# Encoder step on one core: token sums of squares pair by pair, the roots' broadcast ahead of the first ada products, 32-column products side by side

## Chip, cores, metric

The kernel runs on one core of a Trainium2 chip, as one launch. The metric is the device time in microseconds, and the kernel before takes 1043.99 us (median of three runs).

## What is computed

One step of an encoder with three kinds of mixers, for 512 prompt tokens and 64 sample tokens of width 2048, in fp32. What matters here is the beginning:

```python
mod = jax.nn.silu(c) @ w_ada + b_ada
shift, scale, gate = jnp.split(mod, 3, axis=-1)
h = rmsnorm(x, norm_g) * (1.0 + scale[:, None]) + shift[:, None]
proj = h @ w_in
```

`rmsnorm` divides each token by the root of the mean of its 2048 squares. Behind the projection come chunked attention, a state space branch, a pooling branch, a gated output projection and a last norm. The change touches none of these.

## The kernel before, in words

**Layout.** x stands feature-major: 16 blocks of 128 features (`xc`, four tiles of four blocks each) by 576 tokens, prompt first. It is loaded by 8 DMAs of two blocks each on the SP queue. An fp32 product on TensorE shows in the trace as two passes (two MATMUL and two LDWEIGHTS records). Projections are made as three products of rounded halves instead: weights and h are split into a high part and the rest (fp32r), and high x high, rest x high and high x rest are added in PSUM.

**Start (L346 to L399).** Each block of x is squared (ScalarE at L353 and L359, the last block on VectorE), and VectorE adds the squares of the even and the odd blocks into two accumulators `acc` (by the helper `add`, L67). Twelve products of `ident` with x (`warm`, L368), whose result nobody reads, run on TensorE meanwhile. Then TensorE sums over the 128 partitions (`pss`, L373): for each of five groups of 128 tokens, two products with `acc` as the stationary operand and one column of ones as the moving one. `rms_inv` (L100) makes the inverse root with one Newton step. Five diagonal matrices `dg` (L391) times ones spread it over all partitions (`rb`, L393 and L395), and ScalarE copies it to `rstdx` (L398, L399).

**Modulation of block b.** `ada_mm` (L330) multiplies SiLU(c) with 2048 x 256 weights of the modulation in 16 fp32 products. Each takes 32 columns of the array and writes 32 partitions of PSUM; four such column groups run side by side. `ada_sel` copies the four partial sums to SBUF (L336), transposes them (L338) and adds them up on VectorE (L340 to L343). `modulate` makes x times scale times `rstdx` (L76), the sample's h `hs` (L421), the prompt's high part `hh` (L423) and the rest `hl` (L76).

**First tiles (L429 to L443).** Of the input projection six tiles of 128 columns are made block by block while the modulation goes on: tiles 0 to 5 for the prompt (three products each, L436 to L438, into `fA` to `fD`), and "tile 6", the sample's 64 tokens for all six, as four fp32 products of 32 array columns each (`fS`, L442). `F1CUT` cuts the seven tiles of a block into three parts: ahead of the next block's ada products, between these and their selection, and behind it.

**Order.** From L320 to L689 the order on TensorE, SP, VectorE and ScalarE is the one in which the code is written (`manual_schedule`). The instructions ahead of L320 (constants, `ones` at L82, `pre` at L89) are placed among them by the framework's scheduler, and so is what comes behind L689. `pre` loads ScalarE's table for the root ahead of its use.

**Loads.** SP issues the loads of ada weights (2 x 1 MB a block, L189) and of first-tile weights (384 KB a block, L178) two blocks ahead. Two of three blocks use four buffers `ada`, so their loads wait for `ada_mm` of three blocks before.

Of the kernel before, what the change touches and what calls it, by code (L numbers as in the profile page):

```python
# [9 lines left out]
F32 = mybir.dt.float32  # L10
# [22 lines left out]
PRE = 2  # L33
F1CUT = ((6, 0), (1,), (2, 3, 4, 5))
MANUAL = 0
# [4 lines left out]
LASTENG = ("PE", "DVE", "Activation")  # L40
WARM = 12
WLANE = 0
W1POS = 2
# [5 lines left out]
def kernel(ctx, tc, xp, xs, xT, cT, wada_ss, wada_g, bsh, bsc, bgate, ng, wf1, wrest,  # L49
# [27 lines left out]

    # ---------------------------------------------------------------- constants
    ident = const.tile([128, 128], F32, name="ident")
# [8 lines left out]
    pre = const.tile([128, 1], F32, name="pre")  # L88
    A.activation(pre, ones[:, 0:1], AF.Sqrt)  # L89
    xc = [ck(f"xc{c}") for c in range(4)]  # L90
# [9 lines left out]
    def rms_inv(pool, ssq, n, bias, hbias, shape, tag):  # L100
        """1/sqrt(ssq/n + bias), with a Newton step; hbias is -bias/2, bias may be None"""
        v = pool.tile(shape, F32, tag=tag + "v", name="v")
        s = pool.tile(shape, F32, tag=tag + "s", name="s")
        ts(v, ssq, -0.5 / n, hbias, ALU.mult, ALU.add)
        if bias is None:
            A.activation(s, v, AF.Sqrt, scale=-2.0)
        else:
            A.activation(s, ssq, AF.Sqrt, scale=1.0 / n, bias=bias)
        r = pool.tile(shape, F32, tag=tag + "r", name="r")
        V.reciprocal(r, s)  # L110
        mul(s, r, r)
        mul(s, s, v)
        stt(r, s, 1.5, r, ALU.add, ALU.mult)
        return r

    # ---------------------------------------------------------------- PSUM
    psctx = ExitStack()
# [5 lines left out]

    # ---------------------------------------------------------------- weights: loaded ahead, split into high and low
    wsrc = [wrest[r, :, 8 * h:8 * h + 8] for r in range(38) for h in range(2)]
# [34 lines left out]

    # ---------------------------------------------------------------- startup: x, modulation, first tiles
    hh, hl = [], []
# [183 lines left out]
    for b in range(PRE):  # L346
        load_ada(b)
    # 1/rms of each token, on every partition
    acc = [wp.tile([128, NT], F32, tag="wh", name="acc") for _ in range(2)]
    for n in range(16):  # L350
        xv = xc[n // 4][:, n % 4]
        if n < 2:
            A.activation(acc[n], xv, AF.Square)  # L353
        else:
            sq = wp.tile([128, NT], F32, tag=("wl", "wr")[n % 2], name="sq")
            if n == 15 and 1:
                mul(sq, xv, xv)
            else:
                A.activation(sq, xv, AF.Square)  # L359
            if n < 16:  # L360
                add(acc[n % 2], acc[n % 2], sq)
            else:
                acc.append(sq)
    V.tensor_scalar(prm[:, 1], prm[:, 1], 1.0, None, op0=ALU.add)
    # keeps the array's clock up until the sums below
    warm = pp.tile([128, 2, 512], F32, tag="pj", name="warm")
    for n in range(WARM):
        PE.matmul(warm[:, 0, 0:128], ident, xc[3][:, WLANE, 0:128], start=True, stop=True)  # L368
    pss = mtile("pss", (128, 8))
    for t in range(5):  # L370
        t0 = 128 * t if t < 4 else NT - 128
        for n, a in enumerate(acc):
            PE.matmul(pss[:, t:t + 1], a[:, t0:t0 + 128], ones[:, 0:1], start=n == 0, stop=n == len(acc) - 1)  # L373
    ada_mm(0, 0)
    ada_mm(0, 1)
    r = rms_inv(s1, pss[:, 0:5], D, None, -0.5 * EPS, [128, 5], "n")
# [12 lines left out]
    rstdx = s1.tile([128, NT], F32, tag="rstdx", name="rstdx", bufs=1)  # L389
    for t in range(5):  # L390
        V.tensor_scalar(dg[:, t], ident, r[:, t:t + 1], None, op0=ALU.mult)  # L391
        if t < 4:
            PE.matmul(rb[:, 0, 128 * t:128 * t + 128], ones, dg[:, t], start=True, stop=True)  # L393
        else:
            PE.matmul(rb[:, 1, 0:64], ones, dg[:, t, 64:128], start=True, stop=True)  # L395
    split_w(0)
    ada_sel(0)
    A.copy(rstdx[:, NP:NT], rb[:, 1, 0:64])  # L398
    A.copy(rstdx[:, 0:NP], rb[:, 0])  # L399

    fA = pp.tile([128, 2, 512], F32, tag="pj", name="fA")
# [27 lines left out]
    def first_tiles(b, fs):  # L429
# [3 lines left out]
        for f in fs:  # L433
            if f < 6:
                wsl = slice(128 * f, 128 * f + 128)
                PE.matmul(f1p[f], wh[:, wsl], hh[c][:, i, 0:NP], start=f0, stop=False)  # L436
                PE.matmul(f1p[f], wl[:, wsl], hh[c][:, i, 0:NP], start=False, stop=False)
                PE.matmul(f1p[f], wh[:, wsl], hl[c][:, i, 0:NP], start=False, stop=l0)  # L438
            else:
                # the sample tokens token-major: a column group for each half of the tokens and of the features  # L440
                for g in range(4):
                    PE.matmul(fS[32 * g:32 * g + 32], hs[:, 32 * (g // 2):32 * (g // 2) + 32],  # L442
                              w[:, 384 * (g % 2):384 * (g % 2) + 384], start=f0, stop=l0, skip_group_check=True)  # L443
# [3 lines left out]
    for b in range(KT):  # L447
# [4 lines left out]
        if b == KT - 2:  # L452
            for n in range(3):
                w_load()
        first_tiles(b, F1CUT[0])
        if b + 1 < KT:
            ada_mm(b + 1, 0)
            ada_mm(b + 1, 1)
        first_tiles(b, F1CUT[1])
        if b + 1 < KT:  # L460
            ada_sel(b + 1)
            modulate(b + 1)
        if b == KT - 2:
            for n in range(1):
                w_split()
        first_tiles(b, F1CUT[2])
        if b == 0:
# [16 lines left out]

    # a projected tile: pieces (psum view, first token, count)
    def f1_pieces(f):
# [4 lines left out]
    def proj_steps(done):  # L491
        """one projected tile, a yield after each sixteenth; then done(psum)"""
        ps = pp.tile([128, 2, 512], F32, tag="pj", name="pj")
# [21 lines left out]
    def interleave(gens, units, total):  # L515
        """runs the steps of gens with the units spread over the first `total` of them"""
        n, done = 0, 0
# [9 lines left out]

    # ---------------------------------------------------------------- attention
    at = ExitStack()
# [192 lines left out]

    # ---------------------------------------------------------------- S5 branch, with the gates z beside it
    zs = ExitStack()
# [4 lines left out]
    def branch_rstd(tiles, ssq, width, out):  # L729
        """out[:, t] = 1/sqrt(sum over features / width + eps), on every partition"""  # L730
        v, s = tiles
# [24 lines left out]
    def s5_units(q):  # L756
# [3 lines left out]
        def op_x():  # L760
            ER = ck("ER", F32, (128, 2304))
            bc = ER[:, 1728:2240].rearrange("p (z a c) -> p z a c", z=4, a=4)
            for z, src in enumerate((sbr, sbi, scr, sci)):
# [4 lines left out]
                      E=[ER[:, 576 * z:576 * z + 576].rearrange("p (a j) -> p a j", a=4) for z in range(3)])  # L768
            # X[state, s, (g, c)] = a^(3-s) coef b
            X = s5.tile([128, 2, 4, 4, 32], F32, tag="X", name="X")  # L770
# [16 lines left out]
        def op_c():  # L787
            # C[state, tau, (g, c)] = c a^tau (imaginary part negated)
            tA, tB, bc = t_["tA"], t_["tB"], t_["bc"]
# [7 lines left out]
        def op_e(part):  # L797
            # E_j = e^(i phi (j+1)); the third row holds the decay, with resets
            E, tA, tB = t_["E"], t_["tA"], t_["tB"]
# [13 lines left out]
        def op_k():  # L813
            # taps of the chunk's own inputs: K[(f, g, c), tau, (g, c')], the skip added to tap 0
            X, Ct = t_["X"], t_["Ct"]
# [13 lines left out]
        def op_g(fp):  # L829
            # inputs of the chunks, rotated  # L830
            E, tA, tB, XT = t_["E"], t_["tA"], t_["tB"], t_["XT"]
# [73 lines left out]

    # pooling
    cinv = zp.tile([128, 16], F32, name="cinv")
# [135 lines left out]

    # ---------------------------------------------------------------- output projection and final norm
    pf = ctx.enter_context(tc.tile_pool(name="pf", bufs=8, space=PSUM, reuse_waits="tile"))
# [104 lines left out]
    def out_gate(t, po, n, cs=slice(0, 512)):  # L1150
        """x + gate * product"""
        out_mul(t, po, n, cs)
# [6 lines left out]
    def out_sum(t):  # L1159
        """the mean of the first three sums of squares, with eps, and that times -1/2"""  # L1160
        m = 128 if t < 4 else 64
# [10 lines left out]
    def out_scale(t, r, c, act=False):  # L1172
        """columns 512 c on: times r, and in the last group times the gain"""
        xv = xo[t][0:128 if t < 4 else 64, 512 * c:512 * c + 512]
# [22 lines left out]

    # in the last group the tiles end one after the other, the last one in two halves
    po = {t: pf.tile([128, 512], F32, tag="f", name="po2") for t in range(5)}
# [56 lines left out]
def _layout(i):  # L1256
# [31 lines left out]

    # groups g = 2 (4 f + q) + g2 -> partition (g2, state), column (q, f)
    def gs(a):  # L1290
        r = a.reshape((4, 4, 2) + a.shape[1:])          # f q g2 s ...
        return np.moveaxis(r, [2, 3, 1, 0], [0, 1, 2, 3])  # g2 s q f ...

# [68 lines left out]
```

## Time and profile before

| | |
|---|---|
| three runs | 1044.51, 1043.99, 1043.70 us |
| median | 1043.99 us |
| the profiled execution: span from the first to the last instruction | 1042.7 us; no other time of it is given |
| TensorE busy | 1011.0 us |
| VectorE, ScalarE busy | 710.5, 460.3 us |
| mean granted clock of TensorE | 0.993 |

Times in the trace count from the start of the span. A row of the timeline gives the start, the duration, the engine, the line, the operation, what it writes and reads, and how many instructions are merged in it. PE is TensorE, DVE VectorE, ACT ScalarE, SPq the queue of SyncE. The ends of matmuls are modelled, so the spacing of starts says more of their pace than a duration does. The granted clock is a share of 2.4 GHz.

### The profile page before, as it was taken

To read this page: it belongs to the slowest core of one execution; us is meant where nothing else is said; L and a number is where in the kernel's file an instruction comes from. 1 tells how busy PE (TensorE), PEld (TensorE's weight loads), DVE (VectorE), ACT (ScalarE), POOL (GpSimd) and SP (SyncE) were. 2 spreads that over 40 slices of the span, in tenths; PEclk is the share of its full clock that TensorE was granted. 3 is DMA by queue.
4 is the path that set the end of the run, shared out by engine and by line. 5 is a ranking of instruction groups with operands and counts; after the bars stand their busy time and mean duration, and the time that the engine had idled before them with its cause. 6 is when DMAs were issued, how large, how long until landed. Compare 5 with 4: busy or idle time off the path is not lost. (4 is left out here: it accounts for less than half of the span.)

```text
span 1042.7 us, 17908 instructions
## 1 busy us (share of the span) xinstructions
PE 1011.0 (97%) x7048; PEld 904.0 (87%) x7048; DVE 710.5 (68%) x1678; ACT 460.3 (44%) x913; POOL 4.2 (0%) x36
## 2 busy tenths in 40 slices
PE   4999999999999999999999999999999999999996
PEld 3556579999999999999989999998999988888885
DVE  5476777656454655645589797886444669988786
ACT  5232355546344535444653644657453513222325
POOL 0000000000000000000000000000000000000000
PEclk8999999999999999999999999999999999999999
DMA  9998833233232233222212322221322596746525
GB/s 365 411 352 327 325 116 116 89 93 98 80 110 84 87 104 99 72 82 73 66 60 81 92 81 71 76 79 42 102 81 82 172 307 207 227 157 192 151 91 192
DMA packets 51572, 148.44 MB, mean 142 GB/s; under 512 B 9313, under 2 KB 18529, under 8 KB 46817
## 3 DMA queue, kind: packets, MB, share of 16 engines
q1 hardware_dynamic: 51488, 147.31, 42.8%
q8 instruction: 55, 0.90, 0.4%
q14 instruction: 29, 0.23, 0.1%
HBM read 137.75 MB, written 9.53 MB: 141 GB/s over the span
## 5 line engine op out<-in xcount | busy, mean ns | idle before, releaser
L500 PE MATMUL pj<-hh,wh 128*128 128x288 f32 x1344 | 299.0, 304 | 0.5 <-DVE Q L76 0.5
L500 PE MATMUL pj<-hh,wl 128*128 128x288 f32 x1344 | 287.8, 296 | 0.0
L500 PE MATMUL pj<-hl,wh 128*128 128x288 f32 x1344 | 287.3, 295 | 0.0
L500 PEld LDWEIGHTS pj<-hh,wh 128*128 128x128 f32 x1344 | 214.6, 189 | 5.5 <-issue 0.8
L500 PEld LDWEIGHTS pj<-hh,wl 128*128 128x128 f32 x1344 | 216.0, 188 | 0.1
L500 PEld LDWEIGHTS pj<-hl,wh 128*128 128x128 f32 x1344 | 215.7, 188 | 0.1
L146 ACT CAST wh<-w 128x1024 fp32r<-128x1024 f32 x120 | 125.8, 1050 | 198.3 <-PE po L1122 86.2
L70 DVE TENSOR_TENSOR wl<-w,wh 128x1024 fp32r<-128x1024 f32 x120 | 146.6, 1222 | 94.0 <-ACT wh L146 93.0
L1119 PE MATMUL po<-wl,yh 128*128 128x512 f32 (+1 forms) x256 | 99.1, 387 | 0.0
L1120 PE MATMUL po<-wh,yl 128*128 128x512 f32 (+1 forms) x256 | 99.0, 387 | 0.0
L1118 PE MATMUL po<-wh,yh 128*128 128x512 f32 (+1 forms) x256 | 98.7, 387 | 0.0
L76 DVE SCALAR_TENSOR_TENSOR acc<-ada,scT,acc 128x512 f32<-128x512 f32 x120 | 83.0, 744 | 0.5
L621 ACT ACTIVATE P<-P,s 128x128 f32<-128x128 f32 (+4 forms) x80 | 43.3, 541 | 77.2 <-DVE s L620 76.9
L618 DVE CUSTOM_DVE_ANT_0 P<-sps,Tb 128x128 f32<-128x128 f32 (+4 forms) x80 | 36.5, 458 | 36.7 <-PE sps L614 22.6
L1118 PEld LDWEIGHTS po<-wh,yh 128*128 128x128 f32 x256 | 48.1, 188 | 9.9
L1120 PEld LDWEIGHTS po<-wh,yl 128*128 128x128 f32 x256 | 48.1, 188 | 9.8
L1119 PEld LDWEIGHTS po<-wl,yh 128*128 128x128 f32 x256 | 48.1, 188 | 9.8
L622 DVE RECIPROCAL s<-s 128x1 f32<-128x1 f32 (+1 forms) x80 | 12.8, 161 | 43.1 <-ACT P L621 42.4
L623 DVE TENSOR_SCALAR P<-P,s 128x128 f32<-128x128 f32 (+4 forms) x80 | 29.5, 370 | 2.3
L423 ACT ACTIVATE hh<-xc,m 128x512 fp32r<-128x512 f32 (+1 forms) x32 | 15.4, 528 | 34.4 <-DVE xc L76 34.4
L67 DVE TENSOR_TENSOR ssqa<-ssqa,sq 128x576 f32<-128x576 f32 x7 | 5.3, 756 | 35.8 <-ACT sq L666 35.8
L70 DVE TENSOR_TENSOR K<-kv,K 64x704 fp32r<-64x704 f32 x32 | 28.2, 883 | 0.5
(338 smaller groups left out, 1427.0 us busy)
## 6 DMA issues: line engine op xcount, KB each, us to landing
w<-in_wrest_dram SPq DMA_DIRECT2D x84, 512.0 KB, 3.7
ada<-in_wada_ss_dram SPq DMA_DIRECT2D x22, 1024.0 KB, 7.1
w<-in_wout_dram SPq DMA_DIRECT2D x32, 512.0 KB, 4.2
ada<-in_wada_g_dram SPq DMA_DIRECT2D x32, 512.0 KB, 4.4
adac<-in_wada_ss_dram SPq DMA_DIRECT2D x10, 1024.0 KB, 11.2
w<-in_wf_dram SPq DMA_DIRECT2D x16, 384.0 KB, 8.1
xc<-in_xT_dram SPq DMA_DIRECT2D x8, 576.0 KB, 7.3
Tb<-in_ext_dram SPq DMA_DIRECT2D x8, 512.0 KB, 3.9
```

The lines of the kernel that those rows point to most:

```text
L70: V.tensor_tensor(o, a, b, op=ALU.subtract)
L76: V.scalar_tensor_tensor(o, in0=a, scalar=s, in1=b, op0=op0, op1=op1)
L146: A.copy(wh, t)
L423: A.activation(hh[c][:, i, tk], xv[:, tk], AF.Identity, bias=m4[:, t:t + 1])
L500: PE.matmul(ps[:, ch, 0:HC], ws[:, k % 8], hs[c][:, i, HC * ch:HC * ch + HC], start=(k == 0 and first), stop=(k == KT - 1 and last))
L618: V.tensor_tensor_reduce(out=p[0:n, 0:nk], in0=ps[0:n], in1=Tb[0:n, h, ::-1][:, b0:b0 + nk], scale=1.0, scalar=-3.0e38, op0=ALU.add, op1=A ...
L621: A.activation(p[0:n, 0:nk], p[0:n, 0:nk], AF.Exp, bias=s4[0:n, 1:2], accum_out=s4[0:n, 2:3])
L622: V.reciprocal(s4[0:n, 3:4], s4[0:n, 2:3])
L623: V.tensor_scalar(p[0:n, 0:nk], p[0:n, 0:nk], s4[0:n, 3:4], None, op0=ALU.mult)
L1118: PE.matmul(po[t], yh[c][:, ci, s_], wh[:, i], start=f0, stop=False)
L1119: PE.matmul(po[t], yh[c][:, ci, s_], wl[:, i], start=False, stop=False)
L1120: PE.matmul(po[t], yl[c][:, ci, s_], wh[:, i], start=False, stop=l0)
```

## The change

It has three parts and some small ones with them. The squares of two blocks are added to each other at once, and the sum goes to TensorE, pair by pair, as five products with one column of ones, all 8 pairs accumulated in one PSUM tile; the accumulators are gone, and instead of 12 warming products in a row there is one behind each pair. Blocks 5, 10 and 15 are squared on VectorE. The broadcast of the roots comes ahead of the ada products of block 0, with the sample's diagonal first, and the split of the first weights comes behind the selection. `F1CUT` becomes two cuts, one for block 0 and one for the others, in which the sample's products stand directly ahead of the ada products. `pre` no longer reads `ones`.

```diff
-F1CUT = ((6, 0), (1,), (2, 3, 4, 5))
+F1CUT = (((6, 0, 1), (2,), (3, 4, 5)), ((6,), (0,), (1, 2, 3, 4, 5)))
-WARM = 12
-WLANE = 0
+WARM = 1
...
-    A.activation(pre, ones[:, 0:1], AF.Sqrt)
+    V.memset(pre, 1.0)
+    A.activation(pre, pre, AF.Sqrt)
...
-    acc = [wp.tile([128, NT], F32, tag="wh", name="acc") for _ in range(2)]
-    for n in range(16):
-        xv = xc[n // 4][:, n % 4]
-        if n < 2:
-            A.activation(acc[n], xv, AF.Square)
+    pss = mtile("pss", (128, 8))
+    warm = pp.tile([128, 2, 512], F32, tag="pj", name="warm")
+    for n in range(0, 16, 2):
+        sq = []
+        for m in range(n, n + 2):
+            q = wp.tile([128, NT], F32, tag=("wl", "wr")[m % 2], name="sq")
+            xv = xc[m // 4][:, m % 4]
+            if m in (5, 10, 15):
+                mul(q, xv, xv)
             else:
-            sq = wp.tile([128, NT], F32, tag=("wl", "wr")[n % 2], name="sq")
-            if n == 15 and 1:
-                mul(sq, xv, xv)
-            else:
-                A.activation(sq, xv, AF.Square)
-            if n < 16:
-                add(acc[n % 2], acc[n % 2], sq)
-            else:
-                acc.append(sq)
+                A.activation(q, xv, AF.Square)
+            sq.append(q)
+        add(sq[0], sq[0], sq[1])
+        for t in range(5):
+            t0 = 128 * t if t < 4 else NT - 128
+            PE.matmul(pss[:, t:t + 1], sq[0][:, t0:t0 + 128], ones[:, 0:1], start=n + t == 0, stop=n == 14,
+                      skip_group_check=True)
+        for w in range(WARM):
+            PE.matmul(warm[:, 0, 0:128], ident, xc[n // 4][:, n % 4, 0:128], start=True, stop=True)
     V.tensor_scalar(prm[:, 1], prm[:, 1], 1.0, None, op0=ALU.add)
-    warm = pp.tile([128, 2, 512], F32, tag="pj", name="warm")
-    for n in range(WARM):
-        PE.matmul(warm[:, 0, 0:128], ident, xc[3][:, WLANE, 0:128], start=True, stop=True)
-    pss = mtile("pss", (128, 8))
-    for t in range(5):
-        t0 = 128 * t if t < 4 else NT - 128
-        for n, a in enumerate(acc):
-            PE.matmul(pss[:, t:t + 1], a[:, t0:t0 + 128], ones[:, 0:1], start=n == 0, stop=n == len(acc) - 1)
-    ada_mm(0, 0)
-    ada_mm(0, 1)
     r = rms_inv(s1, pss[:, 0:5], D, None, -0.5 * EPS, [128, 5], "n")
...
-    for t in range(5):
+    for t in (4, 0, 1, 2, 3):
         V.tensor_scalar(dg[:, t], ident, r[:, t:t + 1], None, op0=ALU.mult)
...
-    split_w(0)
-    ada_sel(0)
     A.copy(rstdx[:, NP:NT], rb[:, 1, 0:64])
     A.copy(rstdx[:, 0:NP], rb[:, 0])
+    ada_mm(0, 0)
+    ada_mm(0, 1)
+    ada_sel(0)
+    split_w(0)
...
-        first_tiles(b, F1CUT[0])
+        cut = F1CUT[b > 0]
+        first_tiles(b, cut[0])
         if b + 1 < KT:
             ada_mm(b + 1, 0)
             ada_mm(b + 1, 1)
-        first_tiles(b, F1CUT[1])
+        first_tiles(b, cut[1])
...
-        first_tiles(b, F1CUT[2])
+        first_tiles(b, cut[2])
```

The rest of the diff takes out comments.

## Rows read from the trace of the kernel before

**Rows 1.** The page, busy time, share of the span and instructions of each engine.
```profile
PE 1011.0 (97%) x7048; PEld 904.0 (87%) x7048; DVE 710.5 (68%) x1678; ACT 460.3 (44%) x913; POOL 4.2 (0%) x36
```
**Rows 2.** Stretches: length, busy time of each engine, granted clock, DMA share, GB/s.
```profile
39.01:46.41 7.40, 7.40 (x62) 4.50 (x61) 3.68 (x10) 2.04 (x5) 0.00 (x0) 1.00 1.02 417
```
**Rows 3.** Timeline of ScalarE and VectorE, 5 to 9 us.
```profile
5.16 1.25 ACT L353 ACTIVATE acc<-xc 128x576 f32<-128x576 f32 x2 [2.30 <-DMA xc<-in_xT_dram]
...
7.44 1.43 DVE L67 TENSOR_TENSOR acc<-acc,sq 128x576 f32<-128x576 f32 x2 [4.29 <-ACT sq L359]
8.78 0.22 DVE L82 TENSOR_SCALAR onesr<-ident 128x128 fp32r<-128x128 f32 x1
```
**Rows 4.** Timeline of TensorE from its first product to the first sample products.
```profile
13.99 4.39 PE L368 MATMUL warm<-xc,ident 128*128 128x128 f32 x24 [13.99 <-DMA xc<-in_xT_dram]
...
19.27 2.90 PE L373 MATMUL pss<-onesr,acc 128*128 128x1 f32 x18 [0.77 <-DVE acc L67]
22.10 3.64 PE L330 MATMUL pa<-ada,sc 128*32 128x256 f32 x32
25.67 1.94 PE L393 MATMUL rb<-dg,onesr 128*128 128x128 f32 x8
...
27.61 0.39 PE L338 MATMUL pa<-ident,S 128*128 128x128 f32 x2
29.49 0.85 PE L442 MATMUL fS<-w,hs 128*32 128x384 f32 x8 [1.49 <-DVE hs L421]
```
**Rows 5.** Timeline of TensorE in three short stretches: the last passes of each.
```profile
16.90 1.38 PE L368 MATMUL warm<-xc,ident 128*128 128x128 f32 x10
...
20.30 1.87 PE L373 MATMUL pss<-onesr,acc 128*128 128x1 f32 x9
...
20.54 1.63 PE L373 MATMUL pss<-onesr,acc 128*128 128x1 f32 x7
```
**Rows 6.** Stretches of the start, columns as in rows 2.
```profile
19.30:20.50 1.20, 1.20 (x11) 1.20 (x12) 0.00 (x0) 0.00 (x0) 0.00 (x0) 1.00 0.95 385
20.60:23.90 3.30, 3.30 (x28) 2.37 (x31) 1.28 (x8) 0.93 (x2) 0.00 (x0) 0.50 1.04 429
30.80:34.10 3.30, 3.20 (x19) 1.59 (x23) 1.91 (x3) 1.01 (x3) 0.00 (x0) 0.50 1.06 382
```
**Rows 7.** Timeline of VectorE and ScalarE, 22 to 29 us.
```profile
22.20 0.16 DVE L73 TENSOR_SCALAR v<-pss 128x5 f32<-128x5 f32 x1 [2.90 <-PE pss L373]
...
23.47 1.07 DVE L391 TENSOR_SCALAR dg<-ident,r 128x128 f32<-128x128 f32 x5
24.45 0.95 DVE L70 TENSOR_TENSOR w1l<-w,w1h 128x768 fp32r<-128x768 f32 x1
28.11 0.17 DVE L340 TENSOR_REDUCE m<-pa 128x4 f32<-128x16 f32 x1 [2.71 <-ACT rstdx L398]
...
25.80 0.37 ACT L336 COPY S<-pa 128x256 f32<-128x256 f32 x1 [2.48 <-PE pa L330]
```
**Rows 8.** Timeline of TensorE in block 1, from the sample products to the ada products.
```profile
39.01 0.85 PE L442 MATMUL fS<-w,hs 128*32 128x384 f32 x8
...
39.35 0.51 PE L442 MATMUL fS<-w,hs 128*32 128x384 f32 x4
...
39.79 0.50 PE L436 MATMUL fA<-hh,w1h 128*128 128x512 f32 x1
40.12 0.39 PE L437 MATMUL fA<-hh,w1l 128*128 128x512 f32 x1
40.36 0.40 PE L438 MATMUL fA<-hl,w1h 128*128 128x512 f32 x1
40.68 1.93 PE L330 MATMUL pa<-adac,sc 128*32 128x256 f32 x32
```
**Rows 9.** SP's timeline, and the landing of the same loads (tile ada, 27.5 to 31 us).
```profile
27.67 2.80 SPq L189 DMA_DIRECT2D ada<-in_wada_ss_dram  x2
...
DMA to landing us min/median/max: 9.9/9.9/10.0
```

## The prediction

> **What bounds the kernel now.** I read the page's busy times first, then the stretches of time, then the timeline of single engines at the start. TensorE is busy 97% of the span [rows 1]. In one turn of the first loop (the 16 k-blocks that make the modulation and the first six tiles) it is busy for 7.40 of 7.40 us at the full granted clock [rows 2]; I take the other blocks of the loop for its like. So time taken off TensorE in a turn leaves the kernel's time one for one, and a delay ahead of the loop is carried to the end, since nothing behind it starts at a set time. What stands ahead of the loop is a chain, not an engine: x lands, squares, sums, root, broadcast, modulation, first product at 29.49 us [rows 4]. The reader is to see two things there: how fast a pass of TensorE with one moving column goes, and at which clock.
>
> An fp32 product is two passes in the trace. Passes that load 128 columns of weights follow each other every 0.208 us at the slow pace (14 passes of the warming products from 13.99 to 16.90) and every 0.223 us in the last seven passes of the sums (20.54 to 22.10); I use 0.213. At the fast pace it is 0.114 us (nine passes from 19.27 to 20.30) [rows 4, 5]. The pass of a sum moves one column and still takes as long as one that moves 128: the weights set it.
>
> **The clock.** The granted clock was 1.00 while sums ran from 19.3 to 20.5, fell to 0.50 (1.2 of 2.4 GHz) at that point, and stayed at 0.50 from 20.6 to 23.9 although TensorE's row is busy for all of those 3.30 us, first with sums, then with ada products [rows 6]. It had risen behind 2.9 us of warming products that move 128 columns [rows 5]. (The column prints 1.00 from the start of the trace; the pace of the warming passes shows the lower level until 16.9.) So passes of one column neither held nor raised it here.
>
> **The change, part by part.**
>
> 1. Sums on TensorE pair by pair. Removed: 14 additions, two accumulators, 20 passes behind the last addition, 24 warming passes. Added: for each of 8 pairs of squares one addition, 5 products of one column and one warming product, so 12 passes. At the slow pace a pair needs 12 x 0.213 = 2.55 us, at the fast pace 1.37. x brings a pair every 1.47 us (the first is there at 5.16, the seventh at 13.99, both starts released by x's DMA) [rows 3, 4]. At the slow pace TensorE is therefore the bound of the start, and only 2 of 12 passes move 128 columns. By the rows above I expect the slow pace throughout. The first pass needs the ones, written at 8.78 for 0.22 us behind the second addition [rows 3]: start at 9.0. The other end: if the ones come behind the first addition, two squares end at 5.16 + 1.25, an addition takes 0.72, the ones 0.22, so 7.4. I take 9.0, the place it has now. The last pass of a sum is the 94th: 9.0 + 93 x 0.213 = 28.8 us. Now it is at 20.54 + 6 x 0.213 = 21.8 us. **Later by 7.0 us** (5.4 with the early start).
>
> The additions that go from VectorE, the squares that move between ScalarE and VectorE, and the table for the root, whose load no longer has to wait for the ones, cost or bring nothing in this case: TensorE lies behind them. The squares now turn over three buffers each, so the squares of the last pair wait for TensorE to finish the fifth pair (9.0 + 5 x 2.55 = 21.8); a square and an addition later is still ahead of 26.9, when TensorE comes to that pair. Behind a held square on its engine stands nothing but other squares and the root.
>
> 2. Broadcast ahead of the ada products. Now the ada products of block 0 (22.10, 3.64 us) run under the root's chain (22.20 to 23.47), and the split of the first weights (24.45, 0.95 us on VectorE) runs under them too [rows 4, 7]. Afterwards all of it is in a row, from the last pass of the sums: 0.38 to the first VectorE step, 1.27 for the root, 0.33 for the first diagonal and its hand-over (five diagonals take 1.07), 10 passes 2.13, ada products until the copy 3.70 (22.10 to 25.80), copy 0.37, hand-over 0.10, transposes until the reduction 0.50 (27.61 to 28.11), modulation until the first sample product 1.38 (28.11 to 29.49). The split now stands in VectorE's order between the small parameters and the modulation, which adds its 0.95. Sum 11.1 us, against 29.49 - 21.82 = 7.7 us now: +3.4. If the clock rises as the ada products start, they take 1.93 instead of 3.64 [rows 4, 8]: +1.7. I take the middle, **+2.6**. Loads: SP issues none of its DMAs elsewhere in its order, but the reload of the first ada buffers waits for these products. It goes at 27.67 now, its second half by 30.5, and lands 9.9 later, at 40.4 [rows 9]; its use is at 40.68 + 7.40 = 48.1 [rows 2, 8]. Load and use both move by about 9 us, so the nearly 8 us of slack stay, and the small loads behind it on SP keep theirs.
>
> 3. The 32-column products side by side. In blocks 1 to 14 the sample products (fS) are followed by the ada products at once, without tile 0 between them. What leaves a turn [rows 8]: from fS to fA 0.44 (39.35 to 39.79) against 0.34 between two rounds of fS: 0.10; the first full product 0.33 against 0.24 for the next: 0.09; from fA to pa 0.32 against 0.24: 0.08. Together 0.27, times 14: **-3.8 us**. The hand-over from fS to pa is in no row; it costs between nothing and those 0.27, which would leave no gain. I take nothing, since both sides work in the same form; the Trainium skill (TensorEngine Tiling (Array Packing), Key Properties) has the engine drained by a change of mode and not by a change of tile, and no row here shows that hand-over. The modulation of the next block gets a tile more of cover, so nothing new waits. Block 0 has the order changed without the two groups meeting: 0, give or take 1.0 for where the low clock of 30.8 to 34.1 [rows 6] comes to lie.
>
> Sum: 7.0 + 2.6 - 3.8 = +5.8 us on the span of 1042.7, which gives 1048.5. The page has no other time of that execution; the median of the runs, 1043.99, lies 1.3 above the span, and on it the sum is **1049.8 us**. Own range of this case: down by 1.6 (early start), 0.9 (clock rises early) and 1.0 (block 0) to 1046.3; up by 0.8, 1.0 and half of part 3 to 1053.5.
>
> **Rivals.**
>
> A. Faster: the clock rises early in the sums and stays. TensorE then works without a break from 9.0 on; if it got the high level after as long as the warming products did, 14 passes go at 0.213 (3.0 us) and 79 at 0.114: last pass at 21.0, 0.8 earlier than now. The broadcast is 1.0 and the ada products 1.7 shorter than in part 2: +0.7 instead of +3.4. The 3.3 us at 0.50 in block 0 would be half as long: -1.6. With part 3: -0.8 + 0.7 - 1.6 - 3.8 = -5.5, 1038.5 us. It decides itself at the second or third pair: with the high clock a pair (1.37) keeps up with x. For it: TensorE would be busy from 9 us on, with a warming product in each pair. Against it: the fall at 20.5 in the midst of sums and no rise in the busy 3.3 us behind it [rows 6]. The Trainium skill (TensorE: Matmul & The Clock Gate, Why this matters for your kernels) speaks for it: keep the engine busy without gaps and it reaches the full clock. By that rule the time would be this 1038.5; the rows show a busy engine at 0.50, which is why I give it less. Chance 0.20.
>
> B. No measurable difference: the clock rises half way through the sums. 46 passes at 0.114 instead of 0.213 take 4.6 off: 1045.2. Chance 0.10.
>
> C. The change does not do in part 3 what it says: the form changes within the group cost as much as the two that go. Then 1049.8 + 3.8 = 1053.6. For it: the ada products start anew with other weights, and the passes of a round share their start. Chance 0.07.
>
> **How the numbers follow.** The likeliest case has 0.63. Slower by over 0.2% (2.1 us, about what a measurement of this kernel can tell from no change) is it and C: 0.70. Within 0.2%: 0.10, B. Faster: 0.20, A. The range reaches from 1043.5, which takes in most of B, to 1053.6, the price of C; outside lies A and little else.
>
> **What would show it.** In the profile of the changed kernel: passes of the sums every 0.213 us from about 9 to 29 us, the granted clock not up before the broadcast or the ada products; ada products of block 0 behind the broadcast; the split of block 0 between the parameters and the modulation on VectorE; the first sample product near 39 us; turns of 7.13 us in the loop. Wrong would be: sums every 0.114 us soon after the start, with the last pass near 21 us (A); a loop still at 7.40 (C).

## The result and the profile after

The changed kernel takes 1052.42 us (median of four runs, 1051.75 to 1053.16) against 1043.85 us for the kernel before (four runs: the three above and one more): ratio 1.0086, 95% interval 1.0072 to 1.0101, so **8.6 us slower**. The prediction had 1049.8 us, slower, in a range that holds the result, 2.6 us below it. The profiled execution took 1053.16 us with a span of 1050.9, so 2.3 us of it lie outside the span.

The page of the changed kernel, busy times (against [rows 1]): TensorE is busy 12.4 us longer and runs 52 instructions more. Where that time goes, the timeline below shows.

```profile
PE 1023.4 (97%) x7100; PEld 923.4 (88%) x7100; DVE 708.6 (67%) x1675; ACT 460.8 (44%) x912; POOL 4.2 (0%) x36
```

TensorE's timeline of the changed kernel, from the first sum to the first sample product (against [rows 4]; start, duration, engine, line, operation, tiles, form, count, idle time before and what ended it):

```profile
9.67 2.29 PE L364 MATMUL pss<-onesr,sq 128*128 128x1 f32 x10 [9.67 <-DVE onesr L81]
11.82 0.78 PE L367 MATMUL warm<-xc,ident 128*128 128x128 f32 x2
12.39 2.13 PE L364 MATMUL pss<-onesr,sq 128*128 128x1 f32 x10
...
27.75 2.13 PE L364 MATMUL pss<-onesr,sq 128*128 128x1 f32 x10
29.75 0.78 PE L367 MATMUL warm<-xc,ident 128*128 128x128 f32 x2
31.53 0.69 PE L388 MATMUL rb<-dg,onesr 128*128 128x64 f32 x2 [1.01 <-DVE dg L384]
32.01 2.02 PE L386 MATMUL rb<-dg,onesr 128*128 128x128 f32 x8
33.96 2.91 PE L330 MATMUL pa<-ada,sc 128*32 128x256 f32 x32
37.37 0.44 PE L338 MATMUL pa<-ident,S 128*128 128x128 f32 x2 [0.50 <-ACT S L336]
39.94 0.87 PE L437 MATMUL fS<-w,hs 128*32 128x384 f32 x4 [2.13 <-DVE hs L416]
```

Ten passes of a sum take 2.13 us, 0.213 each, from the first pair to the last. From 9.67 to 30.5 TensorE never waits, and its last sum starts at 29.53 instead of 21.82. ScalarE's squares no longer wait for x but for TensorE to free a buffer, as its timeline shows:

```profile
8.22 0.68 ACT L359 ACTIVATE sq<-xc 128x576 f32<-128x576 f32 x1 [0.21 <-DMA xc<-in_xT_dram]
12.00 1.26 ACT L359 ACTIVATE sq<-xc 128x576 f32<-128x576 f32 x2 [3.09 <-PE pss L364]
```

VectorE's timeline behind the sums (against [rows 7]): the root, the diagonals, and then the split `w1l`, 0.95 us between the small parameters `m` and the modulation, while TensorE waits.

```profile
29.92 0.16 DVE L72 TENSOR_SCALAR v<-pss 128x5 f32<-128x5 f32 x1 [6.12 <-PE pss L364]
...
31.18 1.07 DVE L384 TENSOR_SCALAR dg<-ident,r 128x128 f32<-128x128 f32 x5
37.91 0.17 DVE L340 TENSOR_REDUCE m<-pa 128x4 f32<-128x16 f32 x1 [5.66 <-PE pa L338]
...
38.45 0.95 DVE L69 TENSOR_TENSOR w1l<-w,w1h 128x768 fp32r<-128x768 f32 x1
...
39.63 0.25 DVE L416 TENSOR_SCALAR hs<-xc,m 128x64 f32<-128x64 f32 x1
```

Stretches of the changed kernel, columns as in [rows 2]: one turn of the loop, the stretch at the high clock in the start, the low one behind it, and two low ones in the middle. Times at which the clock rose or fell, here and below, are those of its record in the trace. The record of this execution begins with the rise at 35.98; what the clock was before is told by the pace of the passes.

```profile
57.35:64.42 7.07, 7.07 (x62) 4.67 (x62) 3.92 (x11) 2.17 (x5) 0.00 (x0) 1.00 0.94 352
36.10:39.30 3.20, 1.20 (x18) 0.39 (x10) 1.35 (x4) 1.10 (x2) 0.00 (x0) 1.00 0.71 210
39.50:46.10 6.60, 6.16 (x34) 2.90 (x38) 2.92 (x6) 1.68 (x3) 0.00 (x0) 0.50 0.63 263
541.20:544.50 3.30, 3.30 (x16) 3.30 (x15) 3.30 (x9) 0.00 (x0) 0.00 (x0) 0.50 0.23 53
715.30:718.60 3.30, 3.30 (x16) 3.30 (x15) 3.30 (x5) 0.34 (x3) 0.00 (x0) 0.50 0.32 81
```

A turn takes 7.07 instead of 7.40 us. TensorE's timeline of that turn shows where the 0.33 went (against [rows 8]):

```profile
57.35 0.85 PE L437 MATMUL fS<-w,hs 128*32 128x384 f32 x8
58.02 1.91 PE L330 MATMUL pa<-ada,sc 128*32 128x256 f32 x32
59.85 0.50 PE L431 MATMUL fA<-hh,w1h 128*128 128x512 f32 x1
60.19 0.39 PE L432 MATMUL fA<-hh,w1l 128*128 128x512 f32 x1
```

The **account** between the two traces, in starts of the same products:

| step | changed kernel against before, us | forecast |
|---|---|---|
| the last sum | 29.53 against 21.82: +7.71 | +7.0 |
| from there to the first sample product | 10.41 against 7.67: +2.74 | +2.6 |
| block 0 | 10.36 against 9.52: +0.84 | 0, give or take 1.0 |
| 14 turns of the loop | 98.92 against 103.63: -4.72 | -3.8 |
| so the last block starts later by | +6.57 | +5.8 |
| hand-over to attention: four transposes that stood there with a wait of 0.45 now run later | -0.62 | no term |
| two low stretches in the middle, and 0.50 that comes back between them | +1.52, +1.24, -0.50 | no term |
| the end of the span | +8.16 | +5.8 |

The steps add up to 8.21; the last 0.05 lie in differences too small for a row.

### The profile page after: what moved, and what is told of

The parts are those of the page before. It is cut to its first block, busy times and chain, and to the rows that moved or that the text cites. A ratio compares the mean times of both kernels' runs of the same rounds, so it can differ in the third digit from the quotient of the medians.

```text
span 1050.9 us, 18005 instructions
## 1 busy us (share of the span) xinstructions
PE 1023.4 (97%) x7100; PEld 923.4 (88%) x7100; DVE 708.6 (67%) x1675; ACT 460.8 (44%) x912; POOL 4.2 (0%) x36
## 5 line engine op out<-in xcount | busy, mean ns | idle before, releaser
L619 DVE TENSOR_SCALAR P<-P,s 128x128 f32<-128x128 f32 (+4 forms) x80 | 29.5, 370 | 2.3
```

Source lines behind the costliest of these rows:

```text
L619: V.tensor_scalar(p[0:n, 0:nk], p[0:n, 0:nk], s4[0:n, 3:4], None, op0=ALU.mult)
```

## The experiments

**The parts alone.** Three kernels, each the kernel before with one part of the change.

`e1_cuts`, the new cuts alone:

```diff
-F1CUT = ((6, 0), (1,), (2, 3, 4, 5))
+F1CUT = (((6, 0, 1), (2,), (3, 4, 5)), ((6,), (0,), (1, 2, 3, 4, 5)))
```

> The kernel before with the new cuts alone (32-column products side by side; sums and broadcast as before). My theory: each turn of the loop from block 1 on goes from 7.40 to 7.07 us, as in the changed kernel, 14 turns, so 4.6 us less, and block 0 is as before or up to 1 us longer: 1039 to 1040.5 us against 1043.9. Rival: the gain of the loop is given back behind it (a load or an evacuation is late next): turns of 7.07 and a time of 1043 to 1044.

Measured: 1040.16 us (1037.84 to 1043.5), ratio to before 0.9967 (0.9951 to 0.9982), 3.7 us faster. The turns are at 7.07 us as in the changed kernel, so the cuts alone make that gain. Of the loop's 4.7 us 3.7 arrive by the medians; two low stretches in the middle cost the traced execution 1.45 and 1.60 us (see below). Its trace starts better than that of the kernel before, though nothing there was changed:

```profile
17.71 2.34 PE L368 MATMUL warm<-xc,ident 128*128 128x128 f32 x10
19.85 2.44 PE L373 MATMUL pss<-onesr,acc 128*128 128x1 f32 x20
22.21 1.93 PE L330 MATMUL pa<-ada,sc 128*32 128x256 f32 x32
```

Twenty passes of the sums start within 2.18 us (19.85 to 22.03), 0.115 each, and the ada products take 1.93 instead of 3.64 [rows 4]: the clock rose at 20.14 and did not fall again in the loop. The same code can start at either pace, and the kernel before with it.

`e2_sums`, the pair sums alone (with one warming product a pair and the new `pre`; the order behind them as before):

```diff
+        add(sq[0], sq[0], sq[1])
+        for t in range(5):
+            PE.matmul(pss[:, t:t + 1], sq[0][:, t0:t0 + 128], ones[:, 0:1], start=n + t == 0, stop=n == 14,
...
+    ada_mm(0, 0)
+    ada_mm(0, 1)
     r = rms_inv(s1, pss[:, 0:5], D, None, -0.5 * EPS, [128, 5], "n")
```

> The kernel before with the sums pair by pair alone (with the constant for the root's table; ada products of block 0 and split where they were before). My theory: TensorE stays at the slow pace, a pair takes 2.56 us, the last pass of the sums is at 29.5 instead of 21.8, and all of these 7.7 us come through: 1050.5 to 1052.5 us. Rival: the late sums are the price of the broadcast's place (which lets TensorE idle and fall), then the sums here end near 21 us and the time is 1043 to 1045.

Measured: 1053.62 us (1051.19 to 1054.34), ratio 1.0089 (1.0066 to 1.0113), 1.1 us above the upper end of the theory and far from the rival. The traced execution is the fastest one, and its mean clock is 0.998; the other three have 0.995 and 1053.0 to 1054.3 us, and where they were at the low level is not seen. In the timeline the sums keep 0.213 us a pass to the end, and the ada products behind them take the 3.64 us of the low level:

```profile
27.98 2.13 PE L363 MATMUL pss<-onesr,sq 128*128 128x1 f32 x10
29.98 0.77 PE L366 MATMUL warm<-xc,ident 128*128 128x128 f32 x2
30.68 3.64 PE L330 MATMUL pa<-ada,sc 128*32 128x256 f32 x32
```

The last sum starts at 29.76, the first sample product at 37.29, 7.8 later than before. This part alone costs as much as the whole change or more (9.8 us by the medians).

`e3_bcast`, the broadcast ahead of the ada products (the sample's diagonal first) and the split behind the selection, alone:

```diff
-    ada_mm(0, 0)
-    ada_mm(0, 1)
     r = rms_inv(s1, pss[:, 0:5], D, None, -0.5 * EPS, [128, 5], "n")
...
-    split_w(0)
-    ada_sel(0)
     A.copy(rstdx[:, NP:NT], rb[:, 1, 0:64])
     A.copy(rstdx[:, 0:NP], rb[:, 0])
+    ada_mm(0, 0)
+    ada_mm(0, 1)
+    ada_sel(0)
+    split_w(0)
```

> The kernel before with the broadcast ahead of the ada products alone, and the first split behind the selection. My theory: the sums end at 21.8 as before, and from there to the first sample product it takes 10.4 us as in the changed kernel instead of 7.7: 1046 to 1047.5 us. Rival: the ada products were not hidden under the root's chain but waited for it in part, then 0 to 1 us more: 1043.9 to 1045.

Measured: 1048.51 us (1048.39 to 1051.99), ratio 1.0055 (1.0035 to 1.0076), 1.0 us above the upper end of the theory. In its timeline TensorE idles 1.65 us for the diagonals, where the ada products used to run, and the first sample product starts at 31.82 instead of 29.49: 2.3 us later.

```profile
23.76 0.69 PE L393 MATMUL rb<-dg,onesr 128*128 128x64 f32 x2 [1.65 <-DVE dg L389]
24.24 2.02 PE L391 MATMUL rb<-dg,onesr 128*128 128x128 f32 x8
26.19 2.56 PE L330 MATMUL pa<-ada,sc 128*32 128x256 f32 x32
...
31.82 0.85 PE L442 MATMUL fS<-w,hs 128*32 128x384 f32 x8 [2.14 <-DVE hs L421]
```

The last block starts 2.8 us later than in the trace of the kernel before, and the span is 3.4 longer. The medians differ by 4.6; of the rest, 1.1 is that the traced execution of the kernel before was slower than its median (worked out in the part on the prediction).

**The parts together.** `e13_sums_bcast` is the changed kernel with the old cuts.

```diff
-F1CUT = (((6, 0, 1), (2,), (3, 4, 5)), ((6,), (0,), (1, 2, 3, 4, 5)))
+F1CUT = (((6, 0), (1,), (2, 3, 4, 5)),) * 2
```

> The changed kernel with the old cuts, so the sums and the broadcast together. Theory (the three parts add up): the turns are at 7.40 us, the rest of the start is as in the changed kernel, the first tile's end comes 14 x 0.33 = 4.7 us later than there, and the time is about 1056 us (1054.3 if no fall of the clock comes in the middle). Rival (the cuts gain from something that the other two parts bring): less than 3 us above the changed kernel, 1055 or under.

Measured: 1056.68 us (1055.62 to 1057.27), ratio to before 1.0120 (1.0100 to 1.0141), 4.3 us above the changed kernel by the medians. Its turns take 7.40, its start is that of the changed kernel (last sum at 29.58, first sample product at 39.86). The theory holds: over 14 turns the cuts give back 4.7 us of a start that is otherwise the same.

**What the sums lack.** `e4_wide` is the changed kernel with 128 moving columns of ones in each product of the sums instead of one. The columns are copies of each other, so the result is the same, and so is the number of passes.

```diff
-            PE.matmul(pss[:, t:t + 1], sq[0][:, t0:t0 + 128], ones[:, 0:1], start=n + t == 0, stop=n == 14,
+            PE.matmul(pss[:, 128 * t:128 * t + 128], sq[0][:, t0:t0 + 128], ones[:, 0:128], start=n == 0 and t in (0, 4),
...
-    r = rms_inv(s1, pss[:, 0:5], D, None, -0.5 * EPS, [128, 5], "n")
+    r = rms_inv(s1, pss[:, 0:513:128], D, None, -0.5 * EPS, [128, 5], "n")
```

> The changed kernel with 128 equal columns of ones as the moving operand of each sum instead of one (same weights, same number of passes; column 0 of each result is used). My theory: passes that move 128 columns let the clock rise in the sums as they did in the kernel before behind the first warming products, a pass then takes 0.11 us, TensorE keeps up with x and the last pass is at 20 to 21.5 us instead of 29.5: 8 to 10 us less than the changed kernel, 1042 to 1044.5 us. Rival: the clock stays low because TensorE waits for x or because the weights are loaded so often, and the time is that of the changed kernel, 1052, or more.

Measured: 1043.44 us (1041.94 to 1044.53), ratio to before 0.9996 (0.9985 to 1.0006), so 9.0 us below the changed kernel by the medians, although the sums move 128 times the columns. Its timeline:

```profile
9.48 2.50 PE L365 MATMUL pss<-onesr,sq 128*128 128x128 f32 x10 [9.48 <-DVE onesr L81]
11.77 0.63 PE L369 MATMUL warm<-xc,ident 128*128 128x128 f32 x2
12.20 1.58 PE L365 MATMUL pss<-onesr,sq 128*128 128x128 f32 x10
...
20.54 1.28 PE L365 MATMUL pss<-onesr,sq 128*128 128x128 f32 x10
...
24.78 1.93 PE L330 MATMUL pa<-ada,sc 128*32 128x256 f32 x32
...
29.78 1.45 PE L439 MATMUL fS<-w,hs 128*32 128x384 f32 x8 [2.13 <-DVE hs L418]
```

At the low level a pass with 128 columns takes the same 0.213 us as one with a single column. In the second pair the pace doubles: the granted clock rose at 12.83, and a pair then takes 1.34 us (12 passes of 0.111). The last sum starts at 21.55 instead of 29.53.

`e5_nowarm` is the changed kernel without the one warming product behind each pair.

```diff
-WARM = 1
+WARM = 0
```

> The changed kernel without the one warming product behind each pair. Theory (the one product of 128 columns in six does nothing for the clock, and its two passes are only two more of 0.213 us): the granted clock stays at 0.50 through the sums as in the changed kernel, a pair takes 10 x 0.213 = 2.13 instead of 2.56 us, seven warming products less ahead of the last sum make its last pass 7 x 0.43 = 3.0 us earlier (26.5 instead of 29.5), and the time is about 1049.4 us. Rival (the warming products hold off something worse, for example the rise of the clock at 35.98 would come later): no gain, 1052 us or more.

Measured: 1050.98 us (1049.23 to 1051.99), ratio to before 1.0071 (1.0056 to 1.0085), 1.4 us below the changed kernel where 3.0 were expected. Up to the loop the theory holds:

```profile
9.77 17.23 PE L364 MATMUL pss<-onesr,sq 128*128 128x1 f32 x80 [9.77 <-DVE onesr L81]
28.64 0.69 PE L388 MATMUL rb<-dg,onesr 128*128 128x64 f32 x2 [1.65 <-DVE dg L384]
```

Eighty passes of 0.213 us, the last at 26.64 (2.9 earlier), and the projection 3.5 earlier than in the changed kernel. In this execution 1.8 us of that go again late: at 830 us TensorE waits 1.46 us for a gate (`z`, ScalarE) ahead of the output products, and the rest comes in the output stage. No other trace shows that wait, and why it came here is open. It is one of six runs, so it does not show why their median is 1.6 us above the expected time.

**The order at the high clock.** `e7_wide_order` is the kernel before with the new cuts and the wide sums of `e4`: the ada products stay under the root's chain and the split under them. Against `e4`:

```diff
-    A.copy(rstdx[:, NP:NT], rb[:, 1, 0:64])
-    A.copy(rstdx[:, 0:NP], rb[:, 0])
-    ada_mm(0, 0)
-    ada_mm(0, 1)
-    ada_sel(0)
     split_w(0)
+    ada_sel(0)
+    A.copy(rstdx[:, NP:NT], rb[:, 1, 0:64])
+    A.copy(rstdx[:, 0:NP], rb[:, 0])
```

(and the two `ada_mm` ahead of `rms_inv` again, and the diagonals from 0 to 4).

> The kernel before with the new cuts and with the sums pair by pair, each with 128 moving columns of ones instead of one; the ada products of block 0 stay ahead of the broadcast, and the split of the first weights behind the diagonals, as before. It tells what the broadcast part costs once the clock is up. Theory (the broadcast part gives its loss at either level, because the ada products no longer run beside the root): the last pass of the sums as in the run with 128 columns and the broadcast first (21.55), the ada products of block 0 at the fast pace under the root's chain, the first sample product near 27.0 us instead of 29.8 there, turns of 7.07; the time about 1036 us, against 1043.4 there. Rival (at the fast pace the ada products are so short, 1.9 us, that their place makes no difference): first sample product at 29 to 30 us, 1042 to 1043 us.

Measured: 1039.26 us (1038.55 to 1039.95), ratio 0.9961 (0.9947 to 0.9975). Better than `e4` by 4.2 us, but 3.3 short of the 1036 expected. Of these, 1.4 lie in the sums: here the clock rose only at 15.54, and the last sum came at 22.91 and not at 21.55. The rest lies in the expected time, which doesn't follow from its own steps: a first sample product at 27.0 instead of 29.8 makes 1040.6 of `e4`'s 1043.4, not 1036. Its timeline:

```profile
21.91 1.28 PE L364 MATMUL pss<-onesr,sq 128*128 128x128 f32 x10
...
28.24 0.85 PE L438 MATMUL fS<-w,hs 128*32 128x384 f32 x8 [1.48 <-DVE hs L417]
```

From the last sum (22.91) to the first sample product it takes 5.33 us; in `e4`, at the same clock, 8.23. So the broadcast part (its place and the split's) costs 2.9 us at the high level too, and the rival falls.

`e8_early_ones` is `e7` with the ones made from a column that a memset fills, not from the identity.

```diff
-    V.tensor_scalar(onesr, ident, 0.0, 1.0, op0=ALU.mult, op1=ALU.add)
+    pre = const.tile([128, 1], F32, name="pre")
+    V.memset(pre, 1.0)
+    V.tensor_scalar(onesr, pre.to_broadcast([128, 128]), 1.0, None, op0=ALU.mult)
```

> The kernel of e7 with the ones written at the start (from a column that a memset fills, instead of from the identity behind the second addition of squares). Theory (with the clock up, the start is bound by x, and what is late is only the first two microseconds of the sums): sums begin at about 7.2 us instead of 9.5, the clock rises some 2 us earlier, the sums catch up with x (one pair in 1.47 us, a pair of sums 1.33), and their last pass is at about 18.5 instead of 21.5 us. The ada weights of block 0, which land at 20.5 us in the run with 128 columns, then become the latest: first sample product at about 25 us, the time 1 to 2.5 us below e7, 1033.5 to 1035 us. Rival (the sums are not what is late, the ada weights already are): the same time as e7.

Measured: **1037.20 us** (1036.11 to 1037.98), ratio to before 0.9939 (0.9925 to 0.9954): the best version, 6.5 us below the kernel before and 15 below the changed one. Its timeline:

```profile
7.46 2.50 PE L364 MATMUL pss<-onesr,sq 128*128 128x128 f32 x10 [7.46 <-DVE sq L66]
...
19.22 1.28 PE L364 MATMUL pss<-onesr,sq 128*128 128x128 f32 x10
20.34 0.39 PE L368 MATMUL warm<-xc,ident 128*128 128x128 f32 x2
20.66 1.93 PE L330 MATMUL pa<-ada,sc 128*32 128x256 f32 x32
...
25.55 0.85 PE L438 MATMUL fS<-w,hs 128*32 128x384 f32 x8 [1.48 <-DVE hs L417]
```

The gain over `e7`, 2.1 us, lies in the expected span; the absolute time is 2.2 above its upper end, since it was counted from the 1036 that `e7` did not reach. The sums did not catch up with x: their last pass is at 20.23, not 18.5, because the two pairs at the low pace are not won back at 1.34 us a pair against 1.47 of x. So the ada weights are not what is latest, if only just: their second half landed at 21.2, and the ada products, which began at 20.66, came to it at 21.5.

`e10_early_nowarm` is `e8` without the warming products (`WARM = 0`).

> The kernel of e8 without the warming product behind each pair. Theory (ten passes with 128 columns a pair raise the clock by themselves, and TensorE waits 0.35 us a pair for x without losing it): as e8 within 0.5 us. Rival (in these gaps the clock falls, or it never rises): passes of 0.213 us in the sums, the last of them 1 to 3 us later, and a time above e8 by 2 to 4 us.

Measured: 1037.90 us (1037.14 to 1039.37), ratio 0.9950 (0.9935 to 0.9964), 0.7 above `e8`: a little over the theory's 0.5, and far from the rival's 2 to 4. In this execution the wide sums needed no warming products: the clock rose at 13.37 and held through them. It fell later, from 27.02 to 30.43, in block 0, which took 9.85 instead of 8.43 us, while the last sum started 0.4 earlier. The ratios' intervals of the two overlap, and one profile doesn't tell whether that fall is the missing products' doing.

**The two low stretches in the middle.** `e11_before_again` and `e12_after_again` are the kernel before and the changed kernel, unchanged, in a second profiled execution.

> The kernel before once more, unchanged, for a second profiled execution. Open is whether the two falls of the clock in the middle (3.41 us each at 0.50, behind the idle gap ahead of km and the one ahead of the branch's sums; +1.5 and +1.2 us) belong to the new cuts. They stand in the traces of the changed kernel and of five of the six experiments with the new cuts (the sixth has the first alone), and in none of the three with the old cuts (the kernel before, the sums alone, the broadcast alone), though the idle gap of 2.33 to 2.41 us ahead of km stands in all ten. Theory (it is chance which execution has them): they can show up here as well. Rival (the old order keeps them away): no fall between 50 and 1030 us here.

> The changed kernel once more, unchanged. Theory (chance): the falls in the middle may be absent, and the span then stands 5.9 us above that of the kernel before, at about 1048.7. Rival (the new cuts bring them): both falls again, span 1050.9.

Measured: 1045.30 us (span 1043.0) and 1051.21 us (span 1048.9), one time each. The kernel before now has a low stretch in the middle too, and the changed kernel has only one of its two. A stretch of each:

```profile
531.40:538.10 6.70, 6.27 (x32) 5.89 (x32) 6.67 (x19) 0.24 (x1) 0.00 (x0) 0.50 0.23 78
```

```profile
715.30:718.60 3.30, 3.30 (x27) 3.30 (x26) 3.30 (x6) 0.06 (x1) 0.00 (x0) 1.00 0.45 138
```

The first is of the kernel before, and adds 2.8 us there; the second is the place of the changed kernel's second low stretch, at 1.00 this time. So the old cuts do not keep them away, and the kernel with the old cuts, `e13`, has the second one as well. That it is chance alone is not shown, though: of the 13 traces the first stretch stands in all eight with the new cuts and in one of the five with the old, the second in six of eight and one of five. The new cuts may make them likelier, and then a part of the loop's gain is lost again there. The second trace of the kernel before tells one more thing: its block 1 starts at 36.85 instead of 39.01, because its low stretch ran from 22.71 to 26.12 only. The changed kernel starts block 1 at 49.90 in its second trace and 50.30 in its first.

## Why the prediction was right, and where it was off

**Part 1, right; 0.7 short.** The pace of 0.213 us and the 12 passes a pair hold in every pair, at the low level of 1.2 GHz: 9.67 + 93 x 0.213 = 29.5, measured 29.53. Only the start was taken too early, 9.0 instead of 9.67. The ones stayed behind the second addition, but with them comes the square of block 5 on VectorE, ahead of them in its order (8.73, 0.75 us). That the low clock is the cause is shown by `e4`, where it rises as in rival A: 9.0 us go with it.

The rows that spoke against rival A were the right ones [rows 6]. In all five traces with pair sums of one column (the changed kernel twice, `e2`, `e5`, `e13`) the clock rises only behind them, at 32.4 to 36.0, although TensorE had worked on them without a break from 9.6 to 9.9 on. In all four with 128 columns it rises among them, at 12.3 to 15.5. That one-column passes do not hold the clock was read from one trace, and is less sure: behind 24 warming passes, the 20 passes of the old sums lose it in the two traces that have a wait of 0.7 to 0.8 us among them (at 20.51, and at 20.68 in `e3`), and run at the high level to their end in the two that have none (`e11`, `e1`). The Trainium skill (TensorE: Matmul & The Clock Gate, Why this matters for your kernels) has the engine reach its full clock if it is kept busy without gaps; here the trace disagrees, with 1.2 GHz through 20 us of products back to back.

**Part 2, right.** +2.74 against +2.6, and +2.3 by itself in `e3`. Its terms were less good than their sum. The ada products took 2.98 us until the copy instead of 3.70, because the clock rose among them (35.98). That rise was not forecast: the value taken was the mean of two cases, and its fit is luck. The broadcast took 2.43 (31.53 to 33.96) instead of 2.13. The split put 0.65 us on the path and not its 0.95: from `m` to the first sample product it takes 2.03 us (37.91 to 39.94) instead of 1.38. No load came late: the loop's turns hold 7.07 without a wait.

**Part 3, right; 0.9 too little.** A turn gained 0.337, not 0.27. The hand-over from `fS` to `pa`, in no row before, is free: from 57.35 to 58.02 are 0.67, two rounds of 0.34. Of the three steps, the first full product gained the 0.09 foreseen, the step out of `fS` 0.11 (0.78 to 0.67), and the one from `fA` 0.09; the rest, 0.04, lies in the ada products themselves (1.87 to 1.83). That agrees with the Trainium skill (TensorEngine Tiling (Array Packing), Key Properties), by which a change of mode drains the engine and a change of tile does not. Rival C is out, since the turns are not at 7.40, and so is B, since no sum of the changed kernel ran at the fast pace in either of its traces.

**Block 0** cost 0.84 where I had 0 give or take 1.0: the low stretch is 6.83 us long here, twice that of before.

**What was off is the base, and what lies behind the loop.** The steps make +6.57 at the start of the last block against +5.8. That this is so near is in part luck: parts 1 and 2 and block 0 came out 0.7, 0.1 and 0.8 longer, and the turns gave back 0.9 more. Behind the loop I let every delay be carried to the end unchanged. In the traces 0.62 us come back at the hand-over, and the low stretches in the middle add 2.3; no term stood for either, and whether these stretches are of the execution or of the new cuts is open.

The base hides another 1.0 us. I set what lies outside the span at 1.3 us by comparing one execution with the median of others; where both times are known it is 2.2 to 2.3 us. So the traced execution of the kernel before took about 1045.0 us (an estimate: 1042.7 + 2.3), 1.1 above the median of 1043.85. The 2.6 us by which the time missed the forecast are thus 2.4 from the traces (8.16 against 5.8) and 1.0 from here, less the 0.7 by which the traced execution of the changed kernel is above its own median. Its start tells why a single trace of this kernel is a weak base: the first sample product, at 29.49 there, comes at 28.47 in the second trace (block 1 then 2.2 us earlier) and at 27.12 in `e1`, where all code ahead of it is the same. The kernel before may or may not find the high clock in its sums; the changed kernel missed it both times.

## What to carry to other kernels

A reduction over partitions with one moving column took as long a pass here as one with 128 columns (0.213 us at the low level), and TensorE stayed at 1.2 GHz for the 20 us that it ran; giving it 128 columns cost nothing at the low level and brought 9 us. When products are moved onto an engine in order to hide them, count their passes at the pace that the profile shows for that form, against the pace at which the data lands. Work that runs under a chain of small dependent steps, like the ada products under the root, was free where it stood, and putting it in a row cost time at either level here (2.3 and 2.9 us). One trace of a kernel whose start depends on when the clock rises is one draw: take a second one before you build a forecast on it. Products that take 32 columns of the array belong side by side: each of the three steps between forms that got shorter gave about 0.1 us a turn.

## What the runs showed that was not expected

- An idle gap of TensorE of only 2.33 to 2.41 us, ahead of `km` in the state space branch, stands in all 13 traces. In 9 of them the clock fell to 0.50 in the gap or at most 1.2 us behind it, in 4 it did not; a stretch at 0.50 cost 1.2 to 1.6 us (2.8 where it was twice as long). At the gap ahead of the branch's sums, 1.72 to 2.20 us, it fell in 7 of 13.
- The first sample product came at 27.12, 28.47 and 29.49 us in three executions of the same code, by where the clock stood as the sums and the ada products ran. With wide sums the times spread less: `e7`'s five runs over 1.4 us and `e4`'s ten over 2.6, against 5.7 for `e1`'s ten.
- Wide sums by themselves bring little over a lucky start: `e7` is 0.9 us below `e1` by the medians, and the fastest run of `e1` (1037.84) is below all of `e7`'s. That their worth is that the clock is up each time fits the four traces, but is not tested further.
- The change to `pre` undid what `pre` is for. It now runs ahead of SiLU's table, and the root's table is loaded once more behind the squares. That costs nothing here, since the root comes 7 us later:

```profile
22.94 1.28 ACT L106 ACT_TABLE_LOAD   x1
```
